# Two sides of SBUF and the expert stage: constants and weight ring moved to the right stack, low parts split by VectorE alone, token pairs summed in PSUM before the add

## The chip, the cores and the metric

One NeuronCore of a Trainium2 chip runs the whole program. The metric is the time of one execution in microseconds (us) on the device; the median of three runs is given, and one more execution was recorded by the hardware profiler.

## The reference, cut to what matters

The input is one sequence of 512 tokens with 1024 features, everything in float32. A first block runs once and a second block twice, one after the other.

```
first_block:   h = x + hybrid_mixer(rms_norm(x))          # 6720 projection columns, two scans, 2048 x 1024 output
               h = h + expert_choice_ffn(rms_norm(h))     # 16 experts, 64 tokens each, 1024 -> 512 -> 1024
               rms_norm(h)
second_block, for l in 0, 1:
               x = x + 0.5 * swiglu(rmsnorm(x))           # 1024 -> 2816 -> 1024
               x = x + attention_mixer(rmsnorm(x))        # 2354 projection columns, 1024 x 1024 output
               x = x + 0.5 * swiglu(rmsnorm(x))
final rmsnorm

expert_choice_ffn: each expert takes the 64 tokens with its highest router weight:
    y_e = (silu(X_e Wgate_e) * (X_e Wup_e)) Wdown_e * weight ;  out[token] += y_e for each of its tokens
```

## The kernel before, in words

**Number format.** Most products are made in three passes of TensorE: every operand is split into a high part (rounded to the reduced float32 of TensorE) and a low part (the rest), and `mm3` (L244 to L250) issues high x high, high x low, low x high into one PSUM bank. In `mm(ps, w, x)` the second argument is the stationary operand (loaded, 128 columns), the third the moving one (streamed, 512 columns). So in the dense stages a weight tile (`whi`, `wlo`) is stationary and the activations (`xh`/`xl` in the gate, up and input projections, `hh`/`hl` in the down projections) move. In the expert stage (`times`, L1532) it is the other way round: 64 gathered tokens with both of their parts (`xg`, `hT`) are stationary and the weight tiles move.

**The weight ring** (`ring`, L206; `weights`, L218). A 512 KB piece of weights is fetched into `raw`, ScalarE writes `whi` from it (L225), VectorE writes `wlo` (L226). There are two buffers of each, 4 KiB of a partition apiece, 24 KiB together. Fetch and split run one piece ahead of TensorE.

**Where things lie in SBUF.** Pools form two stacks: the left one grows upward from the bottom of the 224 KiB of a partition, the right one downward from the top. The bottom 16.1 KiB are taken by the runtime. Before the change the constants (2.8 KiB, L113) come first on the left, then the ring; every other left pool starts above them. Counted from the pool sizes (KiB of a partition):

- constants 16.1 to 18.9; ring 18.9 to 42.9: `raw` 18.9, `whi` 26.9, `wlo` 34.9 and up;
- left pools from 42.9 up: `hh`/`hl` of every feed-forward network (44 tiles of 2 KiB: 42.9 to 130.9 where `xh`/`xl` are on the right, 74.9 to 162.9 above them where they are on the left), `xh`/`xl` of the layer-0 second network, the layer-1 first network and the layer-1 mixer (42.9 to 74.9);
- right pools: `xh`/`xl` of the layer-0 first network, the layer-0 mixer and the layer-1 second network (171.8 to 203.8); `xh`/`xl` of the very first projection (187.8 to 219.8);
- the expert stage: `xg` of the groups 0 and 2 at 58.9 to 74.9, `hT` at 83 to 87, `xg` of the groups 1 and 3 at 93 to 109, the split results `yh`, `yl` at 113 to 121;
- the layer-1 mixer's latent up-projection: its own weight tiles `uqh`, `uql` (stationary) at 113 to 125, `lath`, `latl` (moving) at 125 to 135.

**The order of the work.** Program order on each engine, one queue each. Stages by the profile, in us from the span's start: first projection to 385, scans to 590, output projection to 780, routing and experts to 1135, layer 0 (network 1135 to 1500, mixer to 1835, network to 2190), layer 1 (network to 2550, mixer to 2850, network to 3240). A network is 44 gate and up tiles of 24 matmuls (1056), then 8 output tiles of 66 (528).

**The expert stage** (`moe`, L1499). Weights come as 192 pieces of 512 KB in the order of use. `moe_fetch` (L1463) puts a piece into one of NA `eraw` buffers, one of NC `craw` buffers (early pieces only) or a ring `raw`. `take` (L1506) prepares one piece: every fifth is used unsplit (`NN` = 5); of the others ScalarE writes the high part (L1520), GpSimd the low part of the columns 0 to 320 and VectorE that of the columns 320 to 1024 (L1521 and L1522; the first five pieces GpSimd alone). Half of the split pieces use ring buffers, half the buffers `ehi`, `elo` of their own. `get` keeps four prepared pieces ahead. `inner` makes gate and up of an expert, `turn` transposes, `outer` makes the down product into `ye`, two experts to one tile of 128 rows. After every second expert `back` (L1716) splits `ye` into `yh`, `yl` and makes the 0/1 matrix `PS`, and eight `scatter` steps (L1727) are queued in `extra`: each makes two matmuls into one PSUM bank and VectorE adds the bank to the residual `xT[k]` (L1731). `more` takes one step from `extra` between the weight pieces, on odd turns or when more than eight wait. The last pair's eight steps run after the loop, each followed by `prep2`, which prepares the next network's operands.

Of the kernel before, what the change touches and what calls it, by code (L numbers as in the profile page):

```python
# [10 lines left out]
F = mybir.dt.float32  # L11
R = mybir.dt.float32r
# [3 lines left out]
OP = mybir.AluOpType  # L16
# [6 lines left out]
D = 1024  # L23
# [87 lines left out]
class Net:  # L111
    def __init__(self, tc, a, hc, dbg=None):
        self.tc, self.nc, self.a, self.hc = tc, tc.nc, a, hc  # L113
        self.dbg = dbg or {}
        self.es = ExitStack()
        self.const = self.es.enter_context(tc.tile_pool(name="const", bufs=1))
        self.ps_es = None
        self.psum_cfg(mm=4, aux=4)
        self.pools = [self.const]
        self.xT = [None] * 8  # L120
        self.accs2, self.later = None, []
# [83 lines left out]

    def ring(self, es, raw=2, hi=2, lo=2):  # L206

        self.rp = self.pool(es, "ring")
        self.rb = dict(raw=raw, whi=hi, wlo=lo)
        self.ahead = []  # L210
        self.nlo = 0
# [1207 lines left out]

class MoE:  # L1420

    NA, NC, GW, NN = 9, 8, 320, 5

    AGAIN, LATE = 10, 2

# [71 lines left out]
    def moe(self, before, after):  # L1497
        nc, a = self.nc, self.a
        V, G, S_, P = nc.vector, nc.gpsimd, nc.scalar, nc.tensor  # L1499
# [6 lines left out]
        def take():  # L1506

            i = taken[0]
            taken[0] += 1
            raw = self.moe_raw[i]  # L1510
            if i % self.NN == self.NN - 1:
                ready.append((raw,))
            else:
                n = split[0]
                split[0] += 1
                if n % 4 < 2:
                    hi, lo = self.ring_tile("whi", R, 1, 1024)[:, 0], self.ring_tile("wlo", R, 1, 1024)[:, 0]
                else:
                    hi, lo = (wr.tile([128, 1024], R, name=f"e{n}", bufs=2) for n in ("hi", "lo"))
                S_.copy(hi, raw)  # L1520
                for eng, c in ((G, slice(0, self.GW)), (V, slice(self.GW, 1024))) if i > 4 else ((G, slice(0, 1024)),):  # L1521
                    eng.tensor_tensor(lo[:, c], raw[:, c], hi[:, c].bitcast(F), op=OP.subtract)  # L1522
                ready.append((hi, lo))
            if i == 0:
                for _ in range(self.rb["raw"]):
                    self.moe_fetch()
            if i < self.AGAIN or self.moe_where(i) < 2:
                self.moe_fetch()
# [3 lines left out]
        def times(ps, x, w, cols, first, last):  # L1532
            n = len(w)
            for i in range(n):
                P.matmul(ps, x if n == 2 else x.bitcast(F), w[i][:, cols], start=first and i == 0,  # L1535
                         stop=last and i == n - 1)

        def get():
            while len(ready) < 4 and taken[0] < len(self.moe_seq):
                take()  # L1540
            return ready.popleft()
# [24 lines left out]
        for h in range(2):  # L1566
            c = slice(2 * h, 2 * h + 2)
            V.tensor_tensor(a2[:, :, 32 * h:32 * h + NE], av[:, c], m[:, c].unsqueeze(2).to_broadcast([128, 2, NE]),
                            op=OP.mult)
# [9 lines left out]
        with self.tc.issue_after(done.ins):  # L1579
            for i in range(5):  # L1580
                take()
# [45 lines left out]
        es = ExitStack()  # L1627
        wk = self.pool(es, "moe_wk", side="left")
        late = []
# [34 lines left out]
        def inner(e, m, between):  # L1664

            pa = self.psum("mm")
            for j in range(4):
                w = get()
                if e == 0 and m == 0:
                    gather(0, 2 * j)  # L1670
                    gather(0, 2 * j + 1)
                xe = xg[e // 4][:, :, e % 4].rearrange("p k t s -> p k (t s)")
                for k in range(2):
                    kk = 2 * j + k
                    times(pa, xe[:, kk], w, slice(k * 512, (k + 1) * 512), kk == 0, kk == 7)
                between(j)
            u = wk.tile([128, 512], F, name=f"hu{m}", bufs=1)
            t, u = u[64:128], u[0:64]
            S_.copy(t, pa[64:128, :])
            V.tensor_tensor(u, pa[0:64, :], t, op=OP.add)  # L1680
            hs[e, m] = u
            if m == 0:
                silu = S_.activation(u, u, AF.Silu, scale=re[:, e:e + 1])
                if e == NE - 1:
                    self.log_exp(silu)
            else:
                V.scalar_tensor_tensor(u, u, rv[:, e:e + 1], hs[e, 0], op0=OP.mult, op1=OP.mult)

        def turn(e):
            pt = self.psum("aux")  # L1690
            for k in range(4):
                P.transpose(pt[:, k * 64:(k + 1) * 64], hs[e, 1][:, k * 128:(k + 1) * 128], self.ident[:64, :64])
            hT = hs[e] = wk.tile([128, 4, 2, 64], R, name="hT", bufs=2)
            self.split(hT[:, :, 0], hT[:, :, 1], pt[:, :256].rearrange("p (k s) -> p k s", k=4))

        ys = {}

        def outer(e, between):
            hT = hs[e]
            if e % 2 == 0:  # L1700
                ys[e // 2] = (late[0] if e & 2 else wk).tile([128, D], F, name="ye")
            ye = ys[e // 2]
            py = [self.psum("mm"), self.psum("pn")]
            for j in range(4):
                w = get()
                for hf in range(2):
                    times(py[hf], hT[:, j].rearrange("p t s -> p (t s)"), w, slice(hf * 512, hf * 512 + 512), j == 0,
                          j == 3)
                between(4 + j)
            o = 64 * (e % 2)  # L1710
            for hf in range(2):
                t = ye[o:o + 64, hf * 512:hf * 512 + 512]
                S_.copy(t, py[hf][64:128, :])
                V.tensor_tensor(t, py[hf][0:64, :], t, op=OP.add)

        def back(i):  # L1716

            PS = late[0].tile([128, T], R, name="PS", bufs=2)
            V.tensor_scalar(PS, late[1], ic[:, i:i + 1], None, op0=OP.is_equal)
            yh, yl = (late[0].tile([128, D], R, name=f"y{n}") for n in "hl")  # L1720
            y, ys[i] = ys[i], (PS, yh, yl)
            for hf in range(2):
                s = slice(hf * 512, hf * 512 + 512)
                self.split(yh[:, s], yl[:, s], y[:, s])

        def scatter(i, k):
            PS, yh, yl = ys[i]  # L1727
            ps = self.psum("aux")
            for n, t in enumerate((yh, yl)):
                P.matmul(ps, t[:, k * 128:(k + 1) * 128], PS, start=n == 0, stop=n == 1)  # L1730
            V.tensor_tensor(xT[k], xT[k], ps, op=OP.add)  # L1731

        extra = deque()
# [2 lines left out]
            pass  # L1736

        def more(j):
            if extra and (j % 2 or len(extra) > 8):
                extra.popleft()()  # L1740

        inner(0, 0, nothing)
# [2 lines left out]
        def open_late():  # L1745
            self.moe_first.close()
            late.append(self.pool(es, "moe_late", side="left"))
            late.append(self.hconst(late[0], "rowid"))
            more_tokens(1)

        def more_tokens(g):
            extra.extend((lambda k=k: gather(g, k)) for k in range(8))

        for e in range(NE):
            if e == self.LATE:
                open_late()
            def first(j, e=e):
                if j == 0:
                    turn(e)
                if j == 2 and e and e % 2 == 0:  # L1760
                    i = e // 2 - 1
                    back(i)
                    extra.extend((lambda k=k: scatter(i, k)) for k in range(8))
                more(j)
            if e in (4, 8):
                more_tokens(e // 4 + 1)
            if e + 1 < NE:
                inner(e + 1, 0, first)
                if e == 1 and self.LATE == 1.5:
                    open_late()  # L1770
                inner(e + 1, 1, more)
            else:
                first(0)
            outer(e, more)
        while extra:
            extra.popleft()()
        back(7)
        self.moe_es.close()
        before()
        for k in range(8):  # L1780
            scatter(7, k)
            after(k)
        es.close()
        w0.close()
# [771 lines left out]
```

## Time and profile before

| | |
|---|---|
| median of three runs | 3267.4 us (3254.83, 3267.4, 3268.75) |
| profiled execution, its own time | 3256.5 us |
| its span (first to last instruction) | 3254.8 us |
| TensorE matmul busy | 3114.5 us, 96% |
| VectorE busy | 1894.1 us, 58% |
| ScalarE busy | 1355.6 us, 42% |
| GpSimd busy | 582.9 us, 18% |
| mean granted clock of TensorE | 0.982 of full |

Busy time of TensorE is modelled to the end of each matmul, and matmuls overlap, so 96% says that it is hardly ever without work, not that it works at its peak rate. The rate is read from how many matmuls a stretch of time holds.

### The profile page before, as it was taken

The numbers are of one execution on the slowest core, as the hardware profiler recorded it, in microseconds if no ns is written. First come the engines' busy times: TensorE is split into PE (matmuls) and PEld (weight loads), VectorE is DVE, ScalarE is ACT, GpSimd is POOL, SyncE is SP. The second block draws the span as 40 slices with busy tenths as digits, with TensorE's granted clock in tenths as the row PEclk, the third lists the DMA queues.
The fourth block names the chain that finished last, engine by engine and source line by source line (L and its number), as shares of the span: only waits on it lengthen the run. The fifth ranks groups of instructions, "written<-read, shape, count | busy, mean of one in ns | idle before, by whom it ended". The sixth has DMA issues, their size and how long they took to land.

```text
span 3254.8 us, 39119 instructions
## 1 busy us (share of the span) xinstructions
PE 3114.5 (96%) x14939; PEld 2452.0 (75%) x14939; DVE 1894.1 (58%) x2817; ACT 1355.6 (42%) x2172; POOL 582.9 (18%) x454
## 2 busy tenths in 40 slices
PE   8989998897999899999999999999999999999998
PEld 6867898555665588887776888888888776688887
DVE  6899654554999854435777444334443577644432
ACT  5434433343876632323557323223332345632222
POOL 0000254432766500002220100000001212000000
PEclk9999998898999999999999999999999999999999
DMA  4323301215898533333310333333333331033332
GB/s 119 94 76 107 104 1 50 94 55 175 285 324 311 185 89 95 93 98 90 79 53 8 91 98 97 97 97 96 98 94 96 85 77 50 20 91 97 92 96 84
DMA packets 482537, 336.95 MB, mean 104 GB/s; under 512 B 36079, under 2 KB 428718, under 8 KB 482350
## 3 DMA queue, kind: packets, MB, share of 16 engines
q1 hardware_dynamic: 482350, 334.46, 33.7%
q8 instruction: 118, 1.93, 0.2%
q14 instruction: 69, 0.57, 0.1%
HBM read 324.45 MB, written 9.96 MB: 103 GB/s over the span
## 4 chain that ended last, share of the span: by engine, by line
PE 66%; DVE 5%; issue 3%; POOL 2%; ACT 2%; DMA 0%; POOLq 0%; DVEq 0%; ACTq 0%; SPq 0%
PE mm L248 18%; PE mm L249 18%; PE mm L250 18%; PE mm L1535 3%; PE pn L2257 2%; PE aux L2243 1%; PE aux L1645 1%; DVE sbe L2376 1%; POOL wlo L1522 1%; PE mm L2298 1%; PE mm L2300 1%; PE aux L278 1%; POOL elo L1522 1%; DVE elo L1522 1%; PE aux L2061 0%
## 5 line engine op out<-in xcount | busy, mean ns | idle before, releaser
L225 ACT CAST whi<-raw 128x1024 fp32r<-128x1024 f32 (+1 forms) x395 | 406.9, 1030 | 1249.3 <-PE mm L249 1093.6
L248 PE MATMUL mm<-xh,whi 128*128 128x512 f32 (+1 forms) x2136 | 848.4, 397 | 8.8 <-ACT whi L225 5.0
L250 PE MATMUL mm<-xh,wlo 128*128 128x512 f32 (+1 forms) x2136 | 844.4, 396 | 10.5 <-DVE wlo L226 10.5
L249 PE MATMUL mm<-xl,whi 128*128 128x512 f32 (+1 forms) x2136 | 843.4, 395 | 0.1
L226 DVE TENSOR_TENSOR wlo<-raw,whi 128x1024 fp32r<-128x1024 f32 (+2 forms) x387 | 466.4, 1205 | 300.0 <-ACT whi L225 290.6
L250 PEld LDWEIGHTS mm<-xh,wlo 128*128 128x128 f32 (+1 forms) x2136 | 403.1, 189 | 104.7 <-DVE wlo L226 13.9
L248 PEld LDWEIGHTS mm<-xh,whi 128*128 128x128 f32 (+1 forms) x2136 | 403.3, 189 | 103.5 <-ACT whi L225 9.1
L249 PEld LDWEIGHTS mm<-xl,whi 128*128 128x128 f32 (+1 forms) x2136 | 403.1, 189 | 88.7 <-DVE xl L348 0.5
L269 POOL TENSOR_TENSOR acc<-acc,sq 128x512 f32<-128x512 f32 x46 | 78.2, 1699 | 1556.2 <-ACT sq L266 1250.5
L249 PE MATMUL mm<-hl,whi 128*128 128x512 f32 x704 | 274.6, 390 | 0.0
L248 PE MATMUL mm<-hh,whi 128*128 128x512 f32 x704 | 273.9, 389 | 0.0
L250 PE MATMUL mm<-hh,wlo 128*128 128x512 f32 x704 | 273.9, 389 | 0.0
L481 DVE TENSOR_TENSOR u<-mm,rstd 128x512 f32<-128x512 f32 x88 | 60.8, 691 | 279.6 <-PE mm L250 279.6
L477 DVE TENSOR_TENSOR g<-mm,rstd 128x512 f32<-128x512 f32 x88 | 60.8, 691 | 183.5 <-PE mm L250 182.2
L609 DVE SCALAR_TENSOR_TENSOR cacc<-pad,cw,cacc 128x512 f32<-128x512 f32 x216 | 157.6, 745 | 2.1 <-ACT cacc L605 0.6
L248 PEld LDWEIGHTS mm<-hh,whi 128*128 128x128 f32 x704 | 132.1, 188 | 27.6
L250 PEld LDWEIGHTS mm<-hh,wlo 128*128 128x128 f32 x704 | 132.2, 188 | 27.4
L249 PEld LDWEIGHTS mm<-hl,whi 128*128 128x128 f32 x704 | 132.2, 188 | 27.2
L1522 POOL TENSOR_TENSOR wlo<-eraw,whi 128x320 fp32r<-128x320 f32 x58 | 81.6, 1414 | 52.6 <-ACT whi L1520 41.7
L2203 ACT ACTIVATE Pt<-mm,smst 128x512 f32<-128x512 f32 (+3 forms) x144 | 75.3, 528 | 27.0 <-DVE smst L2202 21.6
L2202 DVE TENSOR_REDUCE smst<-mm 128x1 f32<-128x512 f32 (+3 forms) x144 | 68.8, 481 | 27.0 <-PE mm L2300 14.3
L1522 POOL TENSOR_TENSOR elo<-eraw,ehi 128x320 fp32r<-128x320 f32 x57 | 77.4, 1369 | 36.0 <-ACT ehi L1520 32.3
(676 smaller groups left out, 5050.2 us busy)
## 6 DMA issues: line engine op xcount, KB each, us to landing
raw<-in_ffn_w_gate_dram SPq DMA_DIRECT2D x88, 512.0 KB
raw<-in_ffn_w_up_dram SPq DMA_DIRECT2D x88, 512.0 KB
raw<-in_w_in_dram SPq DMA_DIRECT2D x82, 512.0 KB
raw<-in_ffn_w_down_dram SPq DMA_DIRECT2D x64, 512.0 KB
eraw<-in_w_down_dram SPq DMA_DIRECT2D x52, 512.0 KB
eraw<-in_w_gate_dram SPq DMA_DIRECT2D x48, 512.0 KB
eraw<-in_w_up_dram SPq DMA_DIRECT2D x44, 512.0 KB
raw<-in_w_out_dram SPq DMA_DIRECT2D x32, 512.0 KB
```

The source lines that it names most:

```text
L225: nc.scalar.copy(hi, raw)
L226: (eng or nc.vector).tensor_tensor(lo, raw, hi.bitcast(F), op=OP.subtract)
L248: mm(ps, wh, xh, start=start, stop=False)
L249: mm(ps, wh, xl, start=False, stop=False)
L250: mm(ps, wl, xh, start=False, stop=stop)
L269: (eng or nc.gpsimd).tensor_tensor(acc, acc, s, op=OP.add)
L609: V.scalar_tensor_tensor(ac, pad[:, t:t + T], cw[:, i:i + 1], ac, op0=OP.mult, op1=OP.add)
L1522: eng.tensor_tensor(lo[:, c], raw[:, c], hi[:, c].bitcast(F), op=OP.subtract)
L1535: P.matmul(ps, x if n == 2 else x.bitcast(F), w[i][:, cols], start=first and i == 0, stop=last and i == n - 1)
L2202: V.tensor_reduce(st[:, 0, qc:qc + 1], ps[:, :n], axis=AX.X, op=OP.max, negate=True)
L2203: S_.activation(h.Pt[:, QOFF[qc]:QOFF[qc] + n], ps[:, :n], AF.Exp, bias=st[:, 0, qc:qc + 1], accum_out=st[:, 1, qc:qc + 1])
L2257: P.matmul(po[64 * r:64 * r + 64, kc * 128:], h.v[:, kc], h.PT[:, o:o + 512 - kc * 128], start=start and kc == 0, stop=stop and kc == 3, s ...
```

## The change

The pool of the constants and the ring are opened on the right side, before all others there; so they take the top 26.8 KiB, and both stacks of all other pools lie 26.8 KiB (27,456 bytes) lower. Among themselves the other pools keep their places. The ring then lies at 197.2 to 221.2 KiB (`whi` from 205.2, `wlo` from 213.2); the right-hand `xh`/`xl` at 145.0 to 177.0, the first projection's at 161 to 193.

In the expert stage, the low part of a piece is made by VectorE alone (the first five still by GpSimd alone); there are 8 `eraw` and 9 `craw` buffers in place of 9 and 8; `yh` and `yl` have two buffers; a `scatter` step sums two token pairs (four matmuls) in PSUM, so that it is queued after every fourth expert, and adds once; `more` also takes a step on even turns when more than four wait; the last eight steps, after the loop, do the last two pairs.

```diff
-        self.const = self.es.enter_context(tc.tile_pool(name="const", bufs=1))
+        self.const = self.es.enter_context(tc.tile_pool(name="const", bufs=1, side="right"))
...
-        self.rp = self.pool(es, "ring")
+        self.rp = self.pool(es, "ring", side="right")
...
-    NA, NC, GW, NN = 9, 8, 320, 5
+    NA, NC, NN = 8, 9, 5
...
-                for eng, c in ((G, slice(0, self.GW)), (V, slice(self.GW, 1024))) if i > 4 else ((G, slice(0, 1024)),):
-                    eng.tensor_tensor(lo[:, c], raw[:, c], hi[:, c].bitcast(F), op=OP.subtract)
+                (V if i > 4 else G).tensor_tensor(lo, raw, hi.bitcast(F), op=OP.subtract)
...
-            yh, yl = (late[0].tile([128, D], R, name=f"y{n}") for n in "hl")
+            yh, yl = (late[0].tile([128, D], R, name=f"y{n}", bufs=2) for n in "hl")
...
-        def scatter(i, k):
-            PS, yh, yl = ys[i]
+        def scatter(pairs, k):
             ps = self.psum("aux")
-            for n, t in enumerate((yh, yl)):
-                P.matmul(ps, t[:, k * 128:(k + 1) * 128], PS, start=n == 0, stop=n == 1)
+            n, last = 0, 2 * len(pairs) - 1
+            for i in pairs:
+                PS, yh, yl = ys[i]
+                for t in (yh, yl):
+                    P.matmul(ps, t[:, k * 128:(k + 1) * 128], PS, start=n == 0, stop=n == last)
+                    n += 1
             V.tensor_tensor(xT[k], xT[k], ps, op=OP.add)
...
-            if extra and (j % 2 or len(extra) > 8):
+            if extra and (j % 2 or len(extra) > 4):
...
                     back(i)
-                    extra.extend((lambda k=k: scatter(i, k)) for k in range(8))
+                    if i % 2:
+                        extra.extend((lambda k=k: scatter((i - 1, i), k)) for k in range(8))
...
-            scatter(7, k)
+            scatter((6, 7), k)
```

## Rows read from the trace of the kernel before

**Rows 1.** Page, parts 1 and 4: busy time by engine; the ending chain by line.

```profile
PE 3114.5 (96%) x14939; PEld 2452.0 (75%) x14939; DVE 1894.1 (58%) x2817; ACT 1355.6 (42%) x2172; POOL 582.9 (18%) x454
...
PE mm L248 18%; PE mm L249 18%; PE mm L250 18%; PE mm L1535 3%; PE pn L2257 2%; PE aux L2243 1%; PE aux L1645 1%; DVE sbe L2376 1%; POOL wlo L1522 1%; PE mm L2298 1%; PE mm L2300 1%; PE aux L278 1%; POOL elo L1522 1%; DVE elo L1522 1%; PE aux L2061 0%
```

**Rows 2.** Stretches: length; busy PE, PEld, DVE, ACT, POOL (instructions); clock, DMA share, GB/s.

```profile
1170.00:1370.00 200.00, 200.00 (x862) 162.18 (x861) 94.16 (x114) 58.65 (x72) 0.00 (x0) 1.00 0.32 94
...
2900.00:3100.00 200.00, 200.00 (x862) 162.18 (x861) 90.12 (x108) 57.85 (x71) 0.00 (x0) 1.00 0.33 95
...
2210.00:2410.00 200.00, 200.00 (x884) 165.60 (x883) 92.43 (x112) 59.79 (x74) 0.00 (x0) 1.00 0.34 98
...
2430.00:2540.00 110.00, 110.00 (x487) 91.09 (x486) 34.30 (x36) 29.48 (x36) 10.70 (x6) 1.00 0.35 100
```

**Rows 3.** Timeline of TensorE, latent up-projection, layer 1: start us, duration us, instruction.

```profile
2629.29 0.39 PE L248 MATMUL mm<-lath,uqh 128*128 128x512 f32 x1
...
2634.62 0.40 PE L250 MATMUL mm<-lath,uql 128*128 128x512 f32 x1
```

**Rows 4.** The same view, a down product of an expert.

```profile
882.54 0.39 PE L1535 MATMUL mm<-ehi,hT 128*128 128x512 f32 x1
...
884.41 0.40 PE L1730 MATMUL aux<-PS,yh 128*128 128x512 f32 x1
```

**Rows 5.** The same view, a gate product of an expert.

```profile
813.01 0.39 PE L1535 MATMUL mm<-whi,xg 128*128 128x512 f32 x1
...
815.05 0.39 PE L1535 MATMUL mm<-elo,xg 128*128 128x512 f32 x1
```

**Rows 6.** Stretches as in rows 2: experts, and the tail behind them.

```profile
820.00:1110.00 290.00, 269.68 (x1098) 181.35 (x1099) 264.32 (x328) 209.06 (x270) 191.48 (x143) 0.99 0.86 299
...
1117.00:1136.00 19.00, 16.66 (x66) 12.37 (x66) 18.15 (x23) 14.28 (x24) 9.38 (x6) 0.91 0.16 48
```

**Rows 7.** Groups, 820 to 1110: count | busy us, mean ns | idle before, releasers.

```profile
L1522 POOL TENSOR_TENSOR elo<-eraw,ehi 128x320 fp32r<-128x320 f32 x56 | 75.8, 1365 | 33.3 <-ACT ehi L1520 29.5 <-PE aux L1645 2.2 <-DVE wlo L1522 0.8
...
L1522 DVE TENSOR_TENSOR elo<-eraw,ehi 128x704 fp32r<-128x704 f32 x55 | 58.4, 1073 | 7.2 <-ACT ehi L1520 6.8
...
L1522 DVE TENSOR_TENSOR wlo<-eraw,whi 128x704 fp32r<-128x704 f32 x54 | 57.7, 1071 | 5.2 <-ACT whi L1520 3.5 <-PE mm L1535 1.0 <-DMA raw<-in_w_down_dram 0.3
...
L1731 DVE TENSOR_TENSOR xT<-xT,aux 128x512 f32<-128x512 f32 x54 | 36.1, 677 | 2.4 <-PE aux L1730 2.2
...
L345 DVE TENSOR_TENSOR yl<-ye,yh 128x512 fp32r<-128x512 f32 x14 | 16.9, 1230 | 0.0
...
L1687 DVE SCALAR_TENSOR_TENSOR hu<-hu,rv,hu 64x512 f32<-64x512 f32 x15 | 15.5, 1032 | 0.2
...
L1520 ACT CAST whi<-eraw 128x1024 fp32r<-128x1024 f32 x55 | 56.9, 1048 | 11.0 <-issue 3.6 <-PE mm L1535 2.7 <-PE pn L1535 1.8
...
L1520 ACT CAST whi<-raw 128x1024 fp32r<-128x1024 f32 x12 | 12.5, 1046 | 1.0 <-PE mm L1535 0.6 <-PE pn L1535 0.4
```

**Rows 8.** Single lines: count: shortest/median/longest ns, first and last start, shape.

```profile
L226 DVE TENSOR_TENSOR wlo<-raw,whi x36: 1217/1222/1227, 1173.8 to 1368.4; 128x1024 fp32r<-128x1024 f32 x36
...
L1522 POOL TENSOR_TENSOR elo<-eraw,ehi x56: 855/1517/2274, 820.0 to 1106.9; 128x320 fp32r<-128x320 f32 x56
...
L1522 DVE TENSOR_TENSOR elo<-eraw,ehi x55: 871/893/1570, 819.3 to 1108.0; 128x704 fp32r<-128x704 f32 x55
...
L345 DVE TENSOR_TENSOR yl<-yg,yh x8: 677/682/693, 703.2 to 724.6; 128x512 fp32r<-128x512 f32 x8
...
L1687 DVE SCALAR_TENSOR_TENSOR hu<-hu,rv,hu x16: 735/744/1403, 817.0 to 1103.9; 64x512 f32<-64x512 f32 x16
```

**Rows 9.** Waits of TensorE, 820 to 1110 us: total us, times, longest.

```profile
PE mm L1535 <- POOL elo L1522: 5.8, 12, 0.9
...
PE mm L1535 <- POOL wlo L1522: 5.8, 7, 1.4
...
PE mm L1535 <- DVE elo L1522: 5.5, 9, 1.8
```

## The prediction

> **What bounds the kernel now.** I read the page first: TensorE has work in 96% of the span and its three lines of `mm3` carry 54% of the chain that ended last [rows 1]. So outside the experts and the scans the time is the number of matmuls times their pitch (start to start), and the pitch is the thing to look at. The view by stretches gives it: at full granted clock, with no idle time, 1170 to 1370 us holds 862 matmuls, 232.0 ns each; 2900 to 3100 us again 862; 2210 to 2410 us holds 884, 226.2 ns each; 2430 to 2540 us holds 487, 225.9 ns [rows 2] (one matmul more or less at an edge is 0.3 to 0.5 ns). DMA shares and the other engines' loads are alike. The first two are gate and up products whose moving `xh`/`xl` lie at 171.8 KiB and above; the third is the same code with `xh`/`xl` at 42.9 to 74.9 KiB; the fourth a down product with `hh`/`hl` at 74.9 to 162.9 KiB. All four have their stationary tiles in the ring, at 26.9 to 42.9 KiB. So there are two pitches, 5.8 ns apart, and high moving operands go with the slow one.
>
> The change lowers the moving operands but lifts the stationary ones to 205 to 221 KiB, and the second question is what that does. No dense row of before has a stationary tile above 135 KiB, but three stretches lie between. In the latent up-projection (stationary 113 to 125 KiB, moving 125 to 135) 24 matmuls follow each other without a stall, 23 steps in 5.33 us, 231.7 ns [rows 3]. In a down product of an expert (stationary `hT` at 85 to 86 KiB, moving below 57) eight steps take 1.87 us, 233.8 ns [rows 4]. In a gate product (stationary `xg` at 69 to 74 and 59 to 63 KiB, moving below 57) nine steps take 2.04 us, 226.7 ns [rows 5]. A moving operand at 125 to 135 KiB is not slow by itself, since `hh`/`hl` run through those addresses at 225.9 ns [rows 2]. So the nearest rows say that a stationary tile somewhere above 75 KiB brings the slow pitch too, wherever the moving one lies.
>
> In the expert stage VectorE is busy 264.3 of 290 us, TensorE 269.7, and DMA moves 299 GB/s at 86% of its engines [rows 6]: three resources close together, VectorE's queue in order in front of the other two.
>
> **The placement, step by step.** Stages that are slow now: 2 x 1056 matmuls of gate and up with right-hand `xh`/`xl`, and the layer-0 mixer and first projection. Their moving tiles come down to 145 to 177 KiB (the first projection's to 161 to 193), half of them to where `hh`/`hl` are fast; but their stationary tiles are now high, so by rows 3 they stay at 232: 0.
>
> Stages that are fast now: two whole networks, 2 x 1584 matmuls, and the down products of the other two, 2 x 528: 4224. They go from 226.2 to 232.0 ns, which is 24.5 us, all of it on the path, as TensorE has no idle time there [rows 2]. The layer-1 mixer and the output projection before the experts run at a mixture of the two pitches between stalls; by the loops they have 648 and 384 matmuls; with half of them fast now the loss is 3 us, and I take 2, since stalls hide some: +26 us together. Bounds: above, the highest neighbour, 233.8 ns [rows 4], in place of 232.0 makes 32 us, and if two high operands add (no long row shows it), 5.8 ns more on the 4000 matmuls that are slow now is another 23; below, were the stationary address nothing, the rival A.
>
> ScalarE and VectorE read and write the ring at its new place. ScalarE's cast takes 1046 ns from the low ring and 1048 from `eraw` at 163 to 198 KiB [rows 7], so 0. In the experts the moving ring tiles go high while `xg`, `hT` come down to 32 to 82 KiB; half of the pieces keep the pitch slow that `hT` and the late `xg` make slow now: 0, within 4 us either way (some 600 split matmuls by 5.8 ns).
>
> **VectorE's splits.** Of 141 pieces between 820 and 1110 us (109 from `eraw`, in the two rows shown, 32 from the other buffers), 704 columns take VectorE 1072 ns in the mean [rows 7] though the median is 893; GpSimd's 320 take 1517 in the median and 855 at best [rows 8]. The two slow each other: both read two SBUF operands. The same subtraction over 1024 columns takes VectorE 1222 ns where GpSimd is idle [rows 8]. So a piece costs VectorE 150 ns more: 141 x 0.150 = +21 us. Without GpSimd beside it other two-input work speeds up: `yl` from 1230 to 682 ns (14 times, -7.7 us), the product L1687 from 1032 to 744 (15 times, -4.3 us) [rows 7, 8].
>
> **Two pairs in PSUM.** The matmuls stay 128. Of the adds at 677 ns [rows 7] 54 lie in the window; three groups of eight remain there: -30 x 0.677 = -20.3 us of VectorE. The sum on VectorE is 21 - 7.7 - 4.3 - 20.3 = -11 of 264 us, 4%. What this is worth lies between nothing (TensorE at 269.7 of 290 or DMA takes over) and more than itself: TensorE waits for GpSimd's halves 11.6 us [rows 9], a half that ends 1.5 us after the cast while the whole will end 1.2 after it when VectorE is free; but VectorE is 91% busy, so the piece will often queue behind adds and products, and TensorE behind it. I take -10 us: VectorE's own saving, since it is the fullest in-order queue. Ends: -25 and +12.
>
> In the tail pair 6 now comes with pair 7: 16 matmuls more, 3.7 us of TensorE, where VectorE is busy 18.2 of 19 us [rows 6] and has the same eight adds; TensorE loses those 3.7 us in the loop before. 0 to +2, hidden behind VectorE. One `eraw` buffer less and one `craw` more leaves 10 raw buffers in rotation for 11: a fetch starts one piece later; a piece takes 1.75 us at 299 GB/s [rows 6], so the lead falls from 19 to 17 us: 0. `yh`, `yl` with two buffers take away a wait, not add one.
>
> **Sum.** 26 - 10 = +16 us on the profiled execution's 3256.5, 3272.5. The median of the runs stands 10.9 us above that execution, so 3283 for a median like that of before.
>
> **A rule that speaks against this.** The Trainium skill, SBUF — State Buffer, "Who interferes with whom", says that TensorE never waits on anybody for SBUF, and TensorE: Matmul & The Clock Gate, "Back-to-back issue gap", gives 518 cycles for 512 columns whatever the address, 216 ns. By both the placement would cost and bring nothing. The trace doesn't agree: the same code has 226 and 232 ns at full clock [rows 2]. That rule is rival C.
>
> **Rivals.**
> A. Only the moving address counts, and rows 3 and 4 are slow for another reason (banks alternate in rows 4, latent work on all engines in rows 3). Then 2 x 1056 and the mixer's 456 slow matmuls gain where their tiles come under 161 KiB, half to nearly all of them: 2568 x 5.8 ns = 14.9 us, half to all of it, 10 likely; with the experts' -10 the time is 3247, faster. It decides at the first gate tile of layer 0. For it: rows 2 alone are clean; against: rows 3 and 4 stay slow for as long as they run, and rows 5 are as crowded a stage and fast.
> C. Address is nothing, and what differs between the stretches is something else that stays as it is: only the experts' -10, 3257.
> D. The experts gain more, because GpSimd's halves and VectorE's queue were one chain: -25, and the placement's +26 is cancelled: 3268. DMA allows it: at 86% share [rows 6] the stage could shrink by up to 41 us.
> E. Dearer: two high operands add, or the experts' splits queue on VectorE (+12): 3305.
>
> **How the numbers follow.** Half a per cent, 16 us, is about what a measurement of this kernel can tell from no change. The forecast, 3283, has 0.52 and stands on that edge (0.31 slower, 0.21 the same; its own range 3270 to 3298); A 0.22 (0.18 faster, 0.04 same); C 0.07 (0.01 faster); D 0.11 (0.02 faster); E 0.08, slower. Faster 0.21, same 0.40, slower 0.39. The range takes in most of A and leaves out the outer part of E: 3247 to 3300.
>
> **What would show it.** Stretches in the layer-0 second network and the layer-1 first with about 862 matmuls in 200 us, not 884: the placement costs. With 884 there, and more than 862 in the stretches that are slow now: A. In the experts no GpSimd subtraction after the first five, VectorE's at 1222 ns, 32 adds in place of 64, and the time from the first expert's product to the last add shorter by 10 us. The prediction is wrong if the pitch with a high stationary tile is that of a low one, or if the experts move by more than 25 us.

## The result, and the profile after

The changed kernel takes 3286.33 us in the median (3276.63 to 3289.29, seven runs) beside 3267.40 (3254.83 to 3269.57): a ratio of 1.0059, 95% interval 1.0040 to 1.0077. Its profiled execution took 3279.11 us, span 3277.3. The page's busy times and chain, beside [rows 1]:

```profile
PE 3147.7 (96%) x14939; PEld 2454.6 (75%) x14939; DVE 1880.3 (57%) x2785; ACT 1355.9 (41%) x2172; POOL 378.2 (12%) x304
...
PE mm L250 18%; PE mm L249 18%; PE mm L248 18%; PE mm L1534 4%; PE pn L2261 2%; PE aux L2247 1%; PE aux L1644 1%; PE pn L1534 1%; DVE sbe L2380 1%; DVE elo L1521 1%; PE mm L2302 1%; PE aux L1732 1%; PE aux L278 1%; PE mm L2304 1%; PE aux L2065 0%
```

The same 14939 matmuls keep TensorE busy 33 us longer, and GpSimd's splits are gone from the chain. Stretches after, columns as in [rows 2]: gate and up of the first network, of the third (the first of layer 1), its down product, gate and up of the last network, and the experts:

```profile
1170.00:1370.00 200.00, 200.00 (x859) 160.90 (x858) 89.10 (x108) 59.32 (x72) 0.00 (x0) 1.00 0.32 94
2230.00:2430.00 200.00, 200.00 (x858) 161.03 (x858) 90.71 (x108) 58.64 (x72) 0.00 (x0) 1.00 0.32 93
2450.00:2560.00 110.00, 110.00 (x474) 88.54 (x473) 34.34 (x36) 28.61 (x35) 10.64 (x6) 1.00 0.33 92
2925.00:3125.00 200.00, 200.00 (x859) 160.90 (x858) 89.13 (x107) 57.91 (x71) 0.00 (x0) 1.00 0.32 95
820.00:1100.00 280.00, 266.64 (x1105) 181.33 (x1103) 255.41 (x304) 214.17 (x276) 0.00 (x0) 0.99 0.87 314
```

All dense stretches now hold 858 or 859 matmuls in 200 us (474 in 110) where [rows 2] held 862 or 884 (487), at the full granted clock: one pitch (start to start) of some 233 ns everywhere. In the experts VectorE's splits take what [rows 8] gave for 1024 columns beside an idle GpSimd, and the adds between 820 and 1110 us are half of those in [rows 7]:

```profile
L1521 DVE TENSOR_TENSOR wlo<-eraw,whi 128x1024 fp32r<-128x1024 f32 x69 | 83.2, 1219 | 6.2 <-ACT whi L1520 5.6
...
L1734 DVE TENSOR_TENSOR xT<-xT,aux 128x512 f32<-128x512 f32 x27 | 18.1, 681 | 1.0 <-PE aux L1732 0.6
L1686 DVE SCALAR_TENSOR_TENSOR hu<-hu,rv,hu 64x512 f32<-64x512 f32 x16 | 11.8, 740 | 0.2
```

Waits of TensorE from 820 to 1110 us: GpSimd's 11.6 us of [rows 9] are gone, and VectorE's splits cost 8.9 where they had cost 6.8, 5.5 in [rows 9] and 1.3 in the line of before shown last:

```profile
PE mm L1534 <- DVE elo L1521: 7.0, 13, 0.9
...
PE mm L1534 <- DVE wlo L1521: 1.9, 5, 0.8
```

```profile
PE mm L1535 <- DVE wlo L1522: 1.3, 3, 0.7
```

Lengths of the stages in the profiled executions, from the start of the first to that of the last matmul of a stage, worked out from the traces, one execution each (x: gate and up, h: down; "in phase" is an experiment below; networks 1 and 2 are those of layer 0). The experts are the time from the end of the output projection to the first x:

```
                          before   after   in phase
first projection          364.3    366.0   362.4
experts                   351.5    337.8   337.6
network 1  x / h          256.0 / 119.5   256.9 / 123.0   253.7 / 119.5
network 2  x / h          241.9 / 119.5   248.8 / 123.0   241.9 / 119.5
network 3  x / h          241.9 / 119.5   248.8 / 123.0   241.9 / 119.5
network 4  x / h          247.8 / 123.2   248.8 / 126.0   241.9 / 123.2
```

So the placement costs and the experts gain, both somewhat more than forecast. The next question was whether the reason held.

### The profile page after: what moved, and what is told of

Same layout as the page of the kernel before. It is cut to its first block, busy times and chain, and to the rows that moved or that the text cites. A ratio compares the mean times of both kernels' runs of the same rounds, so it can differ in the third digit from the quotient of the medians.

```text
span 3277.3 us, 38547 instructions
## 1 busy us (share of the span) xinstructions
PE 3147.7 (96%) x14939; PEld 2454.6 (75%) x14939; DVE 1880.3 (57%) x2785; ACT 1355.9 (41%) x2172; POOL 378.2 (12%) x304
## 4 chain that ended last, share of the span: by engine, by line
PE 69%; DVE 5%; ACT 2%; issue 1%; POOL 1%; DMA 0%; DVEq 0%; ACTq 0%; POOLq 0%; SPq 0%
PE mm L250 18%; PE mm L249 18%; PE mm L248 18%; PE mm L1534 4%; PE pn L2261 2%; PE aux L2247 1%; PE aux L1644 1%; PE pn L1534 1%; DVE sbe L2380 1%; DVE elo L1521 1%; PE mm L2302 1%; PE aux L1732 1%; PE aux L278 1%; PE mm L2304 1%; PE aux L2065 0%
## 5 line engine op out<-in xcount | busy, mean ns | idle before, releaser
L250 PE MATMUL mm<-xh,wlo 128*128 128x512 f32 (+1 forms) x2136 | 853.2, 400 | 10.3 <-DVE wlo L226 10.3
L1521 DVE TENSOR_TENSOR wlo<-eraw,whi 128x1024 fp32r<-128x1024 f32 x70 | 84.4, 1220 | 6.2 <-ACT whi L1520 5.6
L2207 ACT ACTIVATE Pt<-mm,smst 128x512 f32<-128x512 f32 (+3 forms) x144 | 75.4, 528 | 26.8 <-DVE smst L2206 21.8
L344 ACT CAST hh<-h 128x512 fp32r<-128x512 f32 x88 | 54.8, 623 | 57.3 <-DVE h L483 57.2
```

The source lines that it names most:

```text
L250: mm(ps, wl, xh, start=False, stop=stop)
L1521: (V if i > 4 else G).tensor_tensor(lo, raw, hi.bitcast(F), op=OP.subtract)
L2207: S_.activation(h.Pt[:, QOFF[qc]:QOFF[qc] + n], ps[:, :n], AF.Exp, bias=st[:, 0, qc:qc + 1], accum_out=st[:, 1, qc:qc + 1])
```

## The experiments

Where a ratio is given, it is to the kernel before, run on the same chip; medians of before were 3259.65 to 3261.75 there. Gains and costs in us are the ratio less 1, times that median.

**One half each.**

```diff
-        self.const = ...tc.tile_pool(name="const", bufs=1))
+        self.const = ...tc.tile_pool(name="const", bufs=1, side="right"))
-        self.rp = self.pool(es, "ring")
+        self.rp = self.pool(es, "ring", side="right")
```

> The kernel before with nothing changed but the side of SBUF: constants and ring on the right, experts as before. Theory W (the weights' address decides the pitch of a dense matmul, wherever the moving operand lies): the whole cost of the change without its gain, +36 us from the lengths of the stages (3303 us for a before of 3267, ratio 1.011), every dense stretch of 200 us holds 857 to 859 matmuls, 233.3 ns each. Rival M (only the moving operand's address counts): dense stretches of 884 and a time of 3257. Rival E (the placement costs nothing, it is the experts' edit that is dear): the time of before, within 5 us.

Measured: 3296.47 us, ratio 1.0115 (1.0099 to 1.0130), +37.5 us. Its third network holds 859 matmuls in 200 us:

```profile
2250.00:2450.00 200.00, 200.00 (x859) 161.15 (x858) 89.27 (x107) 57.79 (x71) 0.00 (x0) 1.00 0.33 95
```

The other half, the change without those two lines:

> The change with the constants and the ring left where they were: only the experts' edits. Theory W: the experts' stage is 14 us shorter as after the change and all else is as before, so 3253 us for a before of 3267, ratio 0.9957; left-hand x and h stretches hold 884 matmuls in 200 us. Rival P (the experts' gain came from the new addresses of xg, hT and the ring, not from the edits): 3267, ratio 1. Rival E: slower than before, 3290.

Measured: 3250.68 us, ratio 0.9965 (0.9952 to 0.9979), -11.4 us. Rivals M, E and P fall. The two add up to +0.8% beside the +0.59% of the whole, within their intervals.

**The weights back on the left.** From the changed kernel:

```diff
         self.rp = self.pool(es, "ring", side="right")
+        self.rl = self.pool(es, "ringl", side="left")
...
-        t = self.rp.tile([128, 1024], dt, name=tag, tag=tag, bufs=self.rb[tag])
+        t = (self.rl if tag in ('whi', 'wlo') else self.rp).tile([128, 1024], dt, name=tag, tag=tag, bufs=self.rb[tag])
```

> The changed kernel, but the split weights whi and wlo back on the left at 16 to 32 KiB; raw weights and constants stay on the right. Theory W: the fast pitch, 226.7 ns, comes back in the left-hand x and h stretches (884 in 200 us), and the right-hand x, now at 161 to 193 KiB, is fast for a part of its tiles: 3248 us for a before of 3267 (3240 to 3254). Rival R (it is the raw ring or the constants on the right, which ScalarE, VectorE and the DMAs touch, that slow the matmuls): the time after the change, 3286, with 858 in 200 us.

Measured: 3247.12 us, ratio 0.9961 (0.9947 to 0.9974). The right-hand x (first line), although its tiles now begin at 161 KiB, is as slow as before; the left-hand x is fast:

```profile
1170.00:1370.00 200.00, 200.00 (x863) 162.17 (x862) 90.57 (x108) 59.87 (x73) 0.00 (x0) 1.00 0.32 94
2200.00:2400.00 200.00, 200.00 (x884) 165.68 (x883) 92.43 (x112) 60.02 (x74) 0.00 (x0) 1.00 0.33 98
```

R falls. The time is the one that W gave, and W is not refuted; but a third of the right-hand tiles now lie below 172 KiB and nothing was gained: a first sign against it.

**An address map.** One engine, no network (the loop, shortened):

```python
def stream(s, m):        # 96 matmuls, in the order of mm3
    for k in range(32):
        h, l = k % 8 * 128, 1024 + k % 8 * 128
        for w, x in ((h, 0), (h, 1024), (l, 512)):
            matmul(acc, t[s][:, w:w + 128], t[m][:, x:x + 512], ...)
```

> The network is left out: TensorE runs streams of 96 fp32r matmuls of 128x512, in the order of mm3, whose stationary and moving tiles are stepped through SBUF in tiles of 8 KiB from 26 to 218 KiB (ta to tx), while no other engine and no DMA works. Theory W: with the moving tile low, 226.7 ns up to a stationary tile at about 75 KiB and 233.3 ns from about 82 KiB on; with the stationary tile low, 226.7 ns up to a moving tile at about 163 KiB and some 232 ns from about 172 KiB on; both high, 233.3 ns and no more. Rival N (the slow pitch needs the other engines' or the DMAs' traffic in SBUF beside it): 226.7 ns in every stream. Rival D (two high operands add): about 239 ns where both are high.

Measured: W falls. Three of 57 streams, as stretches: stationary tile high (tx at 210 KiB), moving high (tw at 202), both high (tv, tx):

```profile
494.00:512.00 18.00, 18.00 (x81) 14.93 (x80) 0.00 (x0) 0.00 (x0) 0.00 (x0) 1.00 0.00 0
950.00:968.00 18.00, 18.00 (x81) 14.89 (x81) 0.00 (x0) 0.00 (x0) 0.00 (x0) 1.00 0.00 1
1145.00:1163.00 18.00, 18.00 (x81) 14.93 (x80) 0.00 (x0) 0.00 (x0) 0.00 (x0) 1.00 0.00 1
```

Every stream runs at 226.7 ns from start to start, worked out from the trace. High addresses are not slow by themselves.

**With a wait, and beside traffic.** The same streams, each begun with a wait for VectorE's copy of the accumulator, and three more beside a queue of other work:

> The network is left out, as in the address map before, where all 57 streams ran at 226.7 ns without one wait between them. Now TensorE waits ahead of every stream of 96 matmuls until VectorE has copied the accumulator out; the tiles (ta at 26 KiB to tw at 202 KiB) are stepped as before. At the end four streams of 192 matmuls with stationary tw follow each other without a wait, beside a queue of ScalarE copies, of VectorE subtractions, of DMAs into SBUF, and beside nothing (moving tc, td, te, tf). Theory H (the pitch has two states; a wait throws TensorE into the slow one, and only low addresses let it come back): 226.7 ns with stationary tiles up to about 75 KiB, 233.3 ns for all 96 from about 82 KiB on; moving tiles from about 172 KiB on slow too; the last four streams fast, or slow from the first disturbance on. Rival N (traffic of other engines or DMAs in SBUF is needed): every stream after a wait 226.7 ns, and one of the three streams beside traffic slow, with the one beside nothing fast. If both come out fast, the cause lies in the network's program and not in addresses or traffic alone.

Measured: 226.7 ns again in every stream once it had settled, and beside traffic too (VectorE busy 36.2 of 38 us, then DMA at 153 GB/s, then 150):

```profile
1265.00:1303.00 38.00, 38.00 (x170) 31.45 (x169) 36.19 (x54) 0.00 (x0) 0.00 (x0) 1.00 0.00 0
1308.00:1346.00 38.00, 38.00 (x169) 31.49 (x168) 0.00 (x0) 0.00 (x0) 0.00 (x0) 1.00 0.49 153
1351.00:1389.00 38.00, 38.00 (x169) 31.46 (x168) 0.00 (x0) 0.00 (x0) 0.00 (x0) 1.00 0.47 150
```

H and N fall both, for tiles that begin as they do in these two maps. (The transfers ran on into the stream that was to have none. ScalarE's copies ran earlier than meant, from 560 to 600 us, beside streams that began with a wait; these too run at 226.7 ns.)

**One of three weights high.** As with the weights on the left, but only whi there:

> The changed kernel with whi back on the left and only wlo on the right at 213 to 221 KiB: of the three matmuls of mm3 one has a high stationary tile. With all three low the time was 3247, with all three high 3286 (beside a before of 3262 to 3267). Theory S (the steady state of a sequence is slow or fast as a whole, one high weight keeps it slow): about 3284, 858 to 862 matmuls in 200 us of the left-hand x. Rival L (each matmul pays for its own weights): a third of the cost, 3260, about 875 in 200 us.

Measured: 3285.53 us, ratio 1.0073 (1.0058 to 1.0088); 859 in 200 us:

```profile
2250.00:2450.00 200.00, 200.00 (x859) 160.78 (x858) 90.16 (x108) 59.20 (x73) 0.00 (x0) 1.00 0.32 93
```

S gave the right time: moving one of the two weight tiles costs 1.12% on the version with both on the left, as much as the whole placement did (1.15%). One of the two weight tiles on the right is as dear as both.

**Phase.** What did the maps have that the network has not? In them all tiles began at 128 bytes modulo 512. In the network they don't. First byte modulo 256, from the allocation of the compiled kernels; the distance is stationary less moving, and two tiles are called in phase where it is 0 (the slices within a tile step by multiples of 256 bytes and change nothing):

```
                          stationary   moving        distance      measured
before, left-hand x, h    ring 192     192             0           884 in 200 us
before, right-hand x      ring 192      64           128           862 in 200 us
before, rows 3            uq   192     32, 192, 32   160, 0, 160   231.7 ns
before, rows 4            hT     0     192            64           233.8 ns
before, rows 5            xg   192     192             0           226.7 ns
after, left-hand x, h     ring 160     128            32           858 in 200 us
after, right-hand x       ring 160       0           160           859 in 200 us
weights left, left x, h   ring 128     128             0           884 in 200 us
weights left, right x     ring 128       0           128           863 in 200 us
```

The constants take 2880 bytes, 64 more than a multiple of 256. On the left they had pushed the ring and the left-hand x up together. With the change all other pools come down by 27,456 bytes, which is 64 modulo 256, and the ring, counted from the top now, goes from 192 to 160, which is 32. So each distance to the ring grew by 32: from 0 to 32 and from 128 to 160. Now a map with tiles 32 bytes longer, which begin at 128, 160, 192, ...:

> The network is left out, as in the two address maps before, where every tile began at 128 bytes modulo 512 and every stream ran at 226.7 ns, high or low, with a wait ahead or without. Now each tile is 32 bytes longer, so that ta, tb, ... begin at 128, 160, 192, ... modulo 512; streams of 96 matmuls with stationary ti and moving ta, stationary ta and moving tj, and both the same. Theory F (phase: what counts is the distance of the stationary tile's address from the moving one's, modulo some power of two up to 512; in the kernel before it is 0 in all fast stretches, 128 in the right-hand x; after the change 32 and 160): 226.7 ns where both are the same tile, wherever it lies, and where the distance is 512 (16 tiles apart, tq with ta); 231 to 234 ns at the distances 32, 64, 128 and 160; a period shorter than 512 would show as more fast streams. Theory W (height): 226.7 ns for all streams, as in the two maps before. Rival T (absolute alignment of either operand to 64 bytes): 226.7 ns at every second tile, also where the distance is 64 or 128.

Measured: theory F, with a period of 256 bytes. Groups of TensorE (out, moving tile, stationary tile; count, busy us, mean ns of one); the distances are 288, 320, 384, 416, 448 and 512 bytes, which is 32, 64, 128, 160, 192 and 0 modulo 256, then one tile as both operands:

```profile
L42 PE MATMUL stall<-ta,tj 128*128 128x512 f32 x96 | 22.6, 396 | 0.9 <-DVE y L47 0.9
...
L42 PE MATMUL stall<-ta,tk 128*128 128x512 f32 x96 | 22.7, 396 | 0.8 <-DVE y L47 0.8
...
L42 PE MATMUL stall<-ta,tm 128*128 128x512 f32 x96 | 22.7, 396 | 0.8 <-DVE y L47 0.8
...
L42 PE MATMUL stall<-ta,tn 128*128 128x512 f32 x96 | 22.6, 396 | 0.9 <-DVE y L47 0.9
...
L42 PE MATMUL stall<-ta,to 128*128 128x512 f32 x96 | 22.3, 393 | 0.8 <-DVE y L47 0.8
...
L42 PE MATMUL stall<-ta,tq 128*128 128x512 f32 x96 | 22.1, 390 | 0.8 <-DVE y L47 0.8
...
L42 PE MATMUL stall<-tw 128*128 128x512 f32 x96 | 22.1, 390 | 0.8 <-DVE y L47 0.8
```

Start to start, mean of the last 55 of each stream, worked out from the same trace; streams with the one tile stepped and those with the other agree to 0.1 ns at equal distance, but for 128, where four of six streams run at 232.4 ns and two (one of each kind) at 233.4:

```
(stationary - moving) modulo 256:    0     32     64     96    128    160    192    224
ns:                              226.7  233.4  233.4  234.3  232.4  233.4  228.9  233.3
```

The eight streams with one tile as both operands run at 226.7 ns wherever it lies, so T falls with W. Nothing else worked beside these streams, VectorE's copies between them apart, and they are slow out of phase: the slow pitch needs no traffic.

**The changed kernel, in phase.** Constants and ring stay on the right:

```diff
     def open_xw(self, es, side=None):
+        n = 8 if side == "left" else 24
+        if n:
+            self.nc.gpsimd.memset(self.pool(es, "phase", side=side).tile([128, n], F, name="phase"), 0.0)
+        self.x_right = side == "right"
...
+        if self.x_right:
+            nc.gpsimd.memset(self.pool(es, "phase", side="left").tile([128, 8], F, name="phase"), 0.0)
         hp = self.pool(es, "ffn_h", side="left")
```

> The changed kernel with constants and ring on the right as they are; the tiles xh, xl, hh, hl of left-hand pools are moved up by 32 bytes and the right-hand xh, xl down by 96, so that stationary and moving tiles of 8862 of the 9378 matmuls of mm3 stand 0 modulo 256 apart (before the shift 32 and 160). Theory F (phase, as in the map with the longer tiles: 226.7 ns at 0, 233.4 ns at 32 and 160): every dense stretch 226.7 ns, 882 to 884 matmuls in 200 us, also in the right-hand x; the stages shorten by 15 (first x), 3 x 7 (the other x), 4 x 3.5 (h) and some 5 in the mixers and first projection, so 3286 - 55 = 3231 us (3222 to 3245). Theory W (high addresses of the weights are slow): 3286 and 858 in 200 us.

Measured: 3230.89 us, ratio 0.9906 (0.9889 to 0.9924). On the changed kernel's 1.0059 that is 1.5%, some 50 us, for spacers of 32 and 96 bytes. The first network's x gives 3 us and not the 15 forecast: its pitch is that of the others (first line below), but I had set it against the second network's length, and its first part has other work and a lower granted clock in this execution (0.84 and 0.81 in two stretches of 20 us from 1100 on; 0.980 over the whole x, 0.993 in the changed kernel). In the next run, with 0.993 there, it takes 250.0 us, 6.9 less than in the changed kernel, as the other networks gain. Right-hand and left-hand x:

```profile
1170.00:1370.00 200.00, 200.00 (x884) 165.62 (x883) 90.92 (x108) 59.74 (x73) 0.00 (x0) 1.00 0.33 97
2200.00:2400.00 200.00, 200.00 (x884) 165.68 (x883) 92.64 (x111) 59.79 (x74) 0.00 (x0) 1.00 0.34 98
```

**Weights left, everything in phase, the experts too.** A spacer of 128 bytes under the right-hand x, and

```diff
-                t = wk.tile([128, 4], F, name="rg", bufs=2)
+                t = wk.tile([128, 32], F, name="rg", bufs=2)[:, :4]
```

which moves hT and xg.

> The kernel with whi and wlo on the left, raw and constants on the right (3247 beside a before of 3262), the right-hand xh, xl moved down by 128 bytes, and in the experts xg and hT by 192, so that all 616 split matmuls of the experts and 9261 of 9378 of mm3 stand 0 modulo 256 apart. Theory F: right-hand x stretches at 226.7 ns, 15 + 6 us off the two stages, 2 to 6 off the first projection and the mixer, and 0 to 4 off the experts, whose matmuls wait: 3247 - 25 = 3222 us (3212 to 3232). Theory W (moving tiles above 172 KiB are slow, and stationary hT and xg above 80): the right-hand x stays at 232 ns, 3247.

Measured: 3230.82 us, ratio 0.9908 (0.9892 to 0.9925), where F had 3222. The pitch of the dense stages is as F says, 884 also in the right-hand x:

```profile
1170.00:1370.00 200.00, 200.00 (x884) 165.68 (x883) 90.20 (x108) 59.83 (x73) 0.00 (x0) 1.00 0.33 97
```

The first network's x had again been put at 15 and gives 7 (257.3 us with the weights left, 250.0 here). The experts' 616 split matmuls in phase give next to nothing, 336.9 us for 337.7 with the weights left; between 820 and 1090 us TensorE still waits 8.9 us there for VectorE's splits, as long as in the changed kernel. This run and the one before are 0.9% faster than the kernel before, by the same.

**The parts of the experts' edit.** Whole splits alone, then pairs alone, then what both brought along (eight eraw, nine craw buffers), each on the kernel before (the second with all that the change does to `scatter`, `more`, `yh` and `yl`, of which the cut shows the queueing):

```diff
-                for eng, c in ((G, slice(0, self.GW)), (V, slice(self.GW, 1024))) if i > 4 else ((G, slice(0, 1024)),):
-                    eng.tensor_tensor(lo[:, c], raw[:, c], hi[:, c].bitcast(F), op=OP.subtract)
+                (V if i > 4 else G).tensor_tensor(lo, raw, hi.bitcast(F), op=OP.subtract)
```

> The kernel before with one edit of the experts: VectorE does whole splits after the first five (buffers eight and nine as in the change); one pair at a time in PSUM. Theory Q (VectorE's queue sets the pace, so its busy time is what counts: +21 for the splits, -12 for what runs faster without GpSimd): 9 us slower than before, ratio 1.003. Rival L (the chain from cast to the end of the later half sets the pace, 11.6 us of TensorE waits for GpSimd): 8 to 12 us faster, ratio 0.997.

```diff
-                    extra.extend((lambda k=k: scatter(i, k)) for k in range(8))
+                    if i % 2:
+                        extra.extend((lambda k=k: scatter((i - 1, i), k)) for k in range(8))
```

> The kernel before with the other edit of the experts alone: two pairs summed in PSUM, half of the adds, GpSimd keeps its 320 columns (eight and nine buffers as in the change). Theory Q: 20 us of VectorE's time go, and with both edits the stage gained 11 to 14, so 15 to 20 us faster, ratio 0.995. Rival L: GpSimd's halves still end last, 0 to 4 us faster, ratio 0.999.

```diff
-    NA, NC, GW, NN = 9, 8, 320, 5
+    NA, NC, GW, NN = 8, 9, 320, 5
```

> The kernel before with eight eraw and nine craw buffers (before nine and eight) and nothing else. Two pairs in PSUM by themselves came with these buffers and were 17.8 us slower than before, whole splits on VectorE with the same buffers 3 us faster. Theory B (the rotation over ten raw buffers in place of eleven costs where GpSimd and VectorE share a split, by putting all the ring's raw pieces with one kind of hi and lo buffer or by the shorter lead of the fetches): 12 to 18 us slower, ratio 1.004 to 1.0055. Rival P (the pairs themselves cost, by bunching matmuls and adds): within 4 us of before.

Measured: splits 3256.58, ratio 0.9987 (0.9977 to 0.9998); pairs 3277.43, 1.0048 (1.0031 to 1.0064); buffers 3265.91, 1.0018 (1.0009 to 1.0027). Neither Q nor L holds for the pairs, and for the buffers neither size: they cost 5.9 us, between B and P. Less that, the splits gain 0.31%, 10 us, by themselves (Q said +9; L's 8 to 12 come only with the buffers taken off), and the pairs lose 0.30%, 10 us, as long as GpSimd shares the splits; once it doesn't, they gain 0.22%, 7 us (0.9965 beside 0.9987, whose intervals just overlap). In the profiled executions the experts' stage takes 357.1 us with the buffers alone, 369.3 with the pairs and 342.4 with the splits. Part of the pairs' loss is to be seen in stretches of the two executions, buffers alone first:

```profile
1020.00:1040.00 20.00, 16.62 (x62) 10.06 (x61) 18.86 (x26) 11.95 (x15) 10.60 (x9) 1.00 0.85 286
1040.00:1060.00 20.00, 17.09 (x57) 9.37 (x55) 15.88 (x18) 13.09 (x17) 14.79 (x11) 1.00 0.91 303
...
1100.00:1120.00 20.00, 17.31 (x60) 10.01 (x60) 17.21 (x23) 12.56 (x16) 10.93 (x9) 1.00 0.51 158
```

then pairs:

```profile
1020.00:1040.00 20.00, 14.63 (x41) 8.47 (x42) 12.01 (x14) 8.66 (x12) 10.51 (x7) 0.83 0.75 257
1040.00:1060.00 20.00, 16.65 (x48) 10.22 (x48) 12.93 (x14) 11.36 (x15) 14.04 (x9) 0.83 0.78 265
...
1100.00:1120.00 20.00, 14.91 (x43) 8.73 (x41) 13.04 (x14) 12.43 (x16) 11.09 (x8) 0.83 0.74 252
```

The granted clock falls to 0.83, a mean of its full and its half level, in three stretches that have it whole in the other run; there 132 matmuls start where 179 did, some 11 us of work at 233 ns. The stretches between catch up a part: from 1000 to 1120 us it is 339 for 370, some 7 us. Before the first fall TensorE waits 1.07 and 1.59 us for VectorE's splits:

```profile
1020.64 0.47 PE L1535 MATMUL mm<-wlo,xg 128*128 128x512 f32 x1 [1.07 <-DVE wlo L1522]
...
1023.38 0.47 PE L1535 MATMUL mm<-elo,xg 128*128 128x512 f32 x1 [1.59 <-DVE elo L1522]
```

Why the pairs make these waits fall together was not settled: it is read from one execution each, and no run holds the clock and halves the adds.

## Why the prediction came out as it did

3283 was forecast and 3286 measured, on the edge of half a per cent where the forecast had put it. The number is right, and the mechanism behind its larger term is not. In part it was luck: the placement was put 11 us too low, the experts' sum came out of wrong parts, and the stages were slow after the move because of where the operands begin modulo 256 bytes. With spacers of 32 and 96 bytes the same move made the kernel faster (0.9906).

- *Two pitches, 5.8 ns apart*: right for [rows 2]; the map shows that the slow one has several levels, from 228.9 to 234.3 ns. In the profiled execution of the placement alone the four networks are 31 us longer, of 40 in all, and that is pitch but for some 2 us in the first x; the rest lies in stages with waits.
- *High moving operands go with the slow one, and a stationary tile somewhere above 75 KiB brings it too*: this step failed. The maps ran at 226.7 ns at every height, and 32 bytes took the slow pitch away with the ring at 205 KiB and above. Height and phase fell together in the rows that were read: the low operands of [rows 2] and [rows 5] were in phase, the high ones of [rows 2], [rows 3] and [rows 4] were not. [Rows 4] stand at 64 bytes and [rows 5] at 0; by the table of distances that gives 233.4 and 226.7 ns for 233.8 and 226.7 in the rows. In [rows 3] two matmuls of three stand at 160 and the third at 0, and the three together are slow, 231.7 ns. The address of a tile in bytes, not in KiB, was the column to look at, and it was to be had before.
- *Fast stages +24.5, slow stages 0, together +26*: measured +37.5 (32 to 42) for the placement alone. Some 3 us are missing because the price was taken from [rows 2], which stand at 128 bytes (232.4 ns in the map), while the change puts the left-hand tiles at 32 (233.4): the fast networks' x lost 6.9 us each and not 6.1, their h 3.5 and not 3.1. The slow stages moved from 128 to 160 bytes, another 1 us for the last network's x, where 0 was forecast. The layer-1 mixer and the output projection, put at 2 together, were 9 us longer in that one execution, the layer-0 mixer 2; the output projection alone differs by up to 5 us between executions that have it at the same addresses.
- *Two high operands may add (in E)*: they don't, since height is nothing.
- *Rival A* falls, since no high moving tile gained by coming down. *Rival D*'s -25 did not come, nor did E's +12. *Rival C*: height is nothing, as it said, but the change moved what counts. By the Trainium skill, TensorE: Matmul & The Clock Gate, "Back-to-back issue gap", 512 columns take 518 cycles, 216 ns, in an isolated gap, and no word there tells of the phase. The nearest that a steady stream here comes is 226.7 ns, 544 cycles at 2.4 GHz, in phase.
- *Experts -10*: measured -11.4; the stage is 11.7 us shorter in the execution with the experts' edit alone, 13.7 in that of the whole change. The sum was right by parts that were wrong. Whole splits were put at +9 of VectorE's time and gained 10 us: GpSimd's half had often been the last to end, as rival D had it and the waits show (11.6 us gone, 2.1 more on VectorE). What part of the gain is VectorE's own speed without GpSimd beside it was not separated. The adds were put at -20 and cost 10 by themselves; the buffers were put at 0 and cost 6. VectorE's busy time was no measure of either: with whole splits alone it is busy 275.0 us of 820 to 1110 where it was 264.3 [rows 6], and the kernel is faster; with the pairs alone 240.7, and it is slower.
- *Durations*: 1222 ns forecast for a split, 1219 measured; yl 685 (682), the product 740 (744), both without GpSimd beside them.
- *Tail 0 to 2*: it lies at the end of the experts' stage and runs into the first network's x; alone it was not measured.

## What to carry to other kernels

Before anything is moved in SBUF, look at where the operands of the dense matmuls begin modulo 256 bytes: with stationary and moving tiles at the same remainder they follow each other 3% faster here (226.7 ns for 233.4), and a spacer of 32 bytes decides it for thousands of them. A pool's odd size (constants of 2880 bytes) shifts whatever stands behind it on that side, so a placement is compared in phase or not at all. And where two theories fit all rows of a trace, a bare loop of the operation with one property stepped tells them apart for the price of one run.

## What the hardware showed that was not expected

The pace of fp32r matmuls of 128x512 at full granted clock depends on the distance of the two operands' addresses modulo 256 bytes: 226.7 ns at 0, 228.9 at 192, 232.4 to 234.3 at the other multiples of 32, alike at all heights tried (26 to 218 KiB at distance 0, 26 to 211 at the others). In the bare loops only distance 0 was tried both with waits and without, and beside other engines' traffic. One matmul of three out of phase costs the sequence as much as three. Out of phase the starts come in a pattern. At distance 32, in the changed kernel's third network, it has a period of two (232, 235, 231, 235 ns from 2300 us on); at 160, in its first network, a period of three, 700 ns for three where 680 is the time in phase:

```profile
1200.02 0.40 PE L250 MATMUL mm<-xh,wlo 128*128 128x512 f32 x1
1200.26 0.39 PE L248 MATMUL mm<-xh,whi 128*128 128x512 f32 x1
1200.49 0.39 PE L249 MATMUL mm<-xl,whi 128*128 128x512 f32 x1
1200.72 0.40 PE L250 MATMUL mm<-xh,wlo 128*128 128x512 f32 x1
```

Why the distance counts stays open.
